# Later result functions, low parts on GpSimd and later mean matmuls in a hybrid encoder layer

## The chip, the cores and the metric

The kernel runs on one core of one Trainium2 chip. The metric is the device time of one execution in microseconds (us). A core has five engines with a queue of instructions each: TensorE (PE in the profile; its weight loads are PEld), VectorE (DVE), ScalarE (ACT), GpSimd (POOL) and SyncE (SP). Each engine works through its own queue in order. Where an instruction needs what another engine or a transfer makes, it waits on a semaphore, and all that stands behind it in the same queue waits too. DMA transfers are issued from queues of SP and GpSimd and run beside the engines.

## What is computed

One encoder layer is applied to two groups of tokens with shared weights: a prompt of 512 tokens and a sample of 1024, both 1024 channels wide, all in float32. Cut to its core:

```python
mod = jax.nn.silu(c) @ w_ada + b_ada
shift, scale, gate = jnp.split(mod[:, None, :], 3, axis=-1)
h = rms_norm(x, g_pre) * (1 + scale) + shift
a_val, a_glu, a_z, u, v, b_z, g_a, g_b = jnp.split(h @ w_in, IN_SPLITS, axis=-1)
# conv branch: GLU, depthwise conv of 31 taps, LayerNorm, gates, projection
y_a = (silu(layer_norm(conv(a_val * sigmoid(a_glu)) + conv_b)) * silu(a_z)) @ conv_proj
# spatial gating branch: per chunk of 128 tokens and channel group
v = layer_norm(gelu(v)); mixed = einsum("gpq,bnqgc->bnpgc", w_s, v) + b_s
y_b = (gelu(u) * mixed * silu(b_z)) @ sgu_proj
m = sigmoid(g_a) * y_a + sigmoid(g_b) * y_b
return x + gate * rms_norm(m @ w_out, g_post)
```

## The kernel before

**Matrix products in three passes.** Every operand of a large product is split into a high part (a rounded copy, `hi`) and a low part (what is left, `lo`), and each product is three matmuls: hi by hi, hi by lo, lo by hi. A weight unit is a tile of 128 x 1024. It is loaded by SP into one of four `raw` buffers; ScalarE copies it into `hi` (line 247). The low part is made in one of two ways. With `by_dma` set, ScalarE writes the negated weight into `lo` (line 250), GpSimd issues a DMA that adds the raw weight to it (line 240), and the `raw` buffer is free when that DMA has landed. Without it, VectorE subtracts (line 259, `unit_dve`). For `hi`, and for `lo` too, there is a ring of four buffers.

**Steps.** The work of TensorE is a list of steps, `steps`, run in the order of the list. A plain step is 24 matmuls of 512 columns. Steps 0 to 87 are the prompt (`CONV_END = 88`): input columns, v (steps 16 to 23), u, the gates, the projections and, as the last eight, the output product with w_out (`steps_o`). Steps 88 to 103 are v of the two sample halves `sa` and `sb` (`steps_v`). Then come 28 pairs of column blocks of the sample, seven steps of 12 matmuls each (`pair`). From step 300 on follow the projections of the sample halves with sproj (`post_B`, two times eight steps), then cproj (`post_A`) and the output (`steps_o`) of each half. The unit's way of making its low part is chosen where the step is made: in `col_step` (line 495), `steps_v` (line 529) and `steps_o` (line 589).

**A pair.** For two column blocks of both halves, seven products of half depth replace eight, in the Winograd form of Strassen's scheme. They go into three banks of PSUM: X (products 0, 2, 4 and 6), Y (product 1) and Z (products 3 and 5). Banks X and Z are added to without being cleared, so what they hold in between is copied out: ScalarE copies X after products 0, 2 and 4 and Z after product 3 (`snap`, line 1014). A product that adds to a bank must wait until the copy of it is done. VectorE adds the copies into three of the four results: C11 after product 1 (line 1018), C22 after product 4 (line 1022), C12 after product 5 (line 1026); the fourth, C21, stays in X. The caller's `finish` applies a sigmoid, GELU or SiLU to a result on ScalarE (lines 1126, 1131, 1148, 1153) and stores it to HBM (`spill`), or, for "um" and "hB", multiplies it on VectorE with an operand that has been stored before (`mul`, line 1158) and is requested some products ahead (`ask`, line 1142). The first eight pairs make the input of the sample's conv (`pair_glu`), whose end is handed over in `finish("end")`.

**The order on the engines.** The order is written out by a planner in the kernel. For each step `s` it emits what follows the step before it, `p`, in this order: `p.a1` (ScalarE: copies or functions), ScalarE's splits of later weights, some background work of VectorE, `p.d1` (VectorE), `p.a2` (ScalarE, after `d1`), background work, `p.d2`, VectorE's splits, then the matmuls of the step, loads of raw weights, `st.extra` (requests), and background work up to the step's end. Before the change a function of C11, C22 or C12 is in `a2` of the product that completes the result, so it stands on ScalarE ahead of the copy in `a1` of the next product. Background work (`bg`, `fill`) is the conv's taps (line 403, 31 for each of eight blocks of the sample, 128 x 1024 each), the normalisations and the splits of their results. The planner keeps a clock for TensorE, VectorE and ScalarE with a cost for each instruction.

**Means.** A normalisation needs the mean over channels, which lie on partitions. `bcast_mean` splits a sum into hi and lo (lines 320 and 321) and multiplies both with a matrix of 1/1024 on TensorE (lines 331 and 332). These two matmuls are not steps; they are put between the matmuls of the steps by `pe_later` at the first place whose planned time is at least `LAG` (1.0 us) after the planned end of the operand. The places are the start of a step and the middle of a plain one (`poll`). After the conv, `late_ln` loads its result again, normalises each sample half and makes hA, the operand of `post_A`: ScalarE's line 1241 makes its high parts, VectorE's line 1232 its low parts. hB, the operand of `post_B`, is made by `hB_gen` (lines 1269 and 1274).

Of the kernel before, what the change touches and what calls it, by code (L numbers as in the profile page):

```python
# [17 lines left out]
F32 = mybir.dt.float32  # L18
# [3 lines left out]
ALU = mybir.AluOpType  # L22
# [18 lines left out]
LAG = 1.0  # L41
PLAIN = 5.25
PROD = PLAIN / 2
CONV_END = 88
# [36 lines left out]
def layer_kernel(ctx: ExitStack, tc, x_p, x_s, xt_p, xt_a, xt_b, par, w_blk, w_v, cproj, sproj, w_out, w_ada, w_gate, wsT, bs,  # L81
# [121 lines left out]
    steps = []  # L203
# [38 lines left out]
    def unit_act(u):  # L242
        if u.hi is None:
            have(u)
            u.hi = part_tile("hi")
            u.lo = part_tile("lo")
            S.copy(u.hi, u.raw)  # L247
            clk["act"] += 0.96
            if u.by_dma:
                S.activation(u.lo, u.raw, AF.Copy, scale=-1.0)  # L250
                clk["act"] += 0.96
                lo_by_dma(u.lo, u.raw)
                u.raw = True
                live["raw"] -= 1
# [50 lines left out]
    def pe_later(lag, cost, fn):  # L305
        box = {}

        def go(now):
            box["b"] = fn()
            box["t"] = now  # L310
        pe_items.append((clk["dve"] + lag, cost, go))
        return box
# [12 lines left out]
    def bcast_mean(src):  # L325

        hi, lo = yield from parts(src)

        def go():
            b = bank()  # L330
            PE.matmul(b, lhsT=onemr, rhs=hi, start=True, stop=False)
            PE.matmul(b, lhsT=onemr, rhs=lo, start=False, stop=True)
            return b
        box = pe_later(LAG, 0.43, go)
        yield from ready(box)
        return box["b"]

# [154 lines left out]
        return st  # L492

    def col_step(t, src, act, a1=None, d1=None, d2=None, a2=None, pre=None, box=None, need=None, by_dma=True):
        u = Unit(src, len(steps), by_dma and (len(steps) < CONV_END or len(steps) % 2 == 0))

        def mm():
            b = bank()
            mm_cols(b, u, act())
            box[0] = b  # L500

        st = add_step(Step(mm, a1, d1, a2, d2, pre, need=need), u)

        def quarter(b, wh, wl, q):
            box[0] = b
            mm_quarter(b, wh, wl, act(), q)
        st.quarter = quarter
        return st
# [15 lines left out]
    def steps_v(t, need=None):  # L524

        for h in range(2):
            banks = []
            for kc in range(4):
                u = Unit(w_v[h, kc], len(steps), len(steps) % 2 == 0)

                def mm(u=u, kc=kc, banks=banks):
                    if kc == 0:
                        banks[:] = [bank() for _ in range(4)]
                    mm_rows(banks, u, t.operand(), kc)

                def a1(h=h, banks=banks):
                    if h == 0:
                        t.v = t.v_home()
                        t.bn = smp.tile([P, 4, 12], F32, tag="bn", name="bn", bufs=1)
                    for i in range(4):  # L540
                        S.activation(t.v[:, i, h * T:(h + 1) * T], banks[i], AF.Gelu_apprx_tanh)

                def d1(h=h):
                    for i in range(4):
                        dv(0.65, lambda: V.bn_stats(out=t.bn[:, i, h * 6:h * 6 + 6], in_=t.v[:, i, h * T:(h + 1) * T]))

                def d2(h=h):
                    if h == 0:
                        return
                    mv = smp.tile([P, 4, 2], F32, tag="mv", name="mv")  # L550
                    for i in range(4):
                        dv(0.15, lambda: V.bn_aggr(out=mv[:, i, :], in_=t.bn[:, i, :].rearrange("p (c s) -> p c s", s=6)))
                    var = smp.tile([P, 4], F32, tag="ss", name="var")
                    dv(0.1, lambda: V.tensor_copy(var, mv[:, :, 1]))
                    r = rstd_small(var, 4, LN_EPS)
                    for i in range(4):
                        dv(0.65, lambda: V.tensor_scalar(t.v[:, i, :], t.v[:, i, :], mv[:, i, 0:1], r[:, i:i + 1],
                                                         op0=ALU.subtract, op1=ALU.mult))
                    if t.after_v:
                        t.after_v()  # L560
                last = kc == 3
                add_step(Step(mm, a1 if last else None, d1 if last else None, None, d2 if last else None,
                              act=2.2 if last else 0.0, need=need if h == 0 and kc == 0 else None), u)
# [20 lines left out]
    def steps_o(t, final, on_end=None):  # L584

        for h in range(2):
            banks = []
            for kc in range(4):
                u = Unit(w_out[h, kc], len(steps), len(steps) < CONV_END or len(steps) % 2 == 0)

                def mm(u=u, h=h, kc=kc, banks=banks):
                    if kc == 0:
                        banks[:] = [bank() for _ in range(4)]
                    if final and h == 1 and kc >= 1:
                        t.wl.append(u)
                        if kc == 3:
                            for i in range(4):
                                for c in (1, 2, 3):
                                    mm_rows(banks, t.wl[c - 1], t.m, c, (i,))
                        return  # L600
                    mm_rows(banks, u, t.m, kc)

                def a1(h=h, kc=kc, banks=banks):
                    if kc == 3:
                        if h == 0:
                            t.o = tok(slot())
                            t.q = smp.tile([P, 2, 4], F32, tag="q", name="q")
                        junk = wk()
                        for i in range(4):
                            S.activation(junk, banks[i], AF.Square, scale=1.0 / 32, accum_out=t.q[:, h, i:i + 1])  # L610

                def d1(h=h, kc=kc, banks=banks):
                    if kc == 3:
                        if h == 1 and final:
                            out_last(t, banks)
                            return
                        c = slice(h * T, h * T + T)
                        for i in range(4):
                            dv(0.6, lambda: V.tensor_mul(t.o[:, i, c], banks[i], G[t.g][:, c]))
                        if h == 1:  # L620
                            bg.insert(0, out_gen(t))
                st = add_step(Step(mm, a1, d1, act=2.3 if kc == 3 else 0.0), u)
                if h == 0 and kc == 0:
                    def start():
                        out_load(t)
                        t.o_begun = True
                    st.extra = start
# [361 lines left out]


    pairs = []

    def pair(src1, src2, finish):

# [16 lines left out]
        def snap(name, of):  # L1011
            def a1():
                st[name] = wk()
                S.copy(st[name], st[of])  # L1014
            return a1
# [16 lines left out]
        mul = getattr(finish, "mul", None)  # L1032
        ask = getattr(finish, "ask", None)

        def times(*what):
            return (lambda: [mul(x) for x in what]) if mul else None

        prod("X", "a", 0, (0, 0), True, False, a1=snap("p1", "X"))
        prod("Y", "a", 1, (0, 1), True, True, d1=d_c11, a2=lambda: finish("C11", st), act=0.0)
        prod("X", "b", 0, "S2", False, False, a1=snap("u2", "X"), d1=times("C11"), need="S")  # L1040
        prod("Z", "b", 1, "S1", True, False, a1=snap("s5", "Z"))
        prod("X", "c", 0, "S3", False, False, a1=snap("u3", "X"), d1=d_c22, a2=lambda: finish("C22", st))
        prod("Z", "c", 1, "S4", False, True, d1=d_c12, a2=lambda: finish("C12", st), need="S4", act=0.0)
        steps[-1].d2 = times("C22")
        prod("X", "d", 0, (1, 1), False, True, a1=lambda: finish("C21", st),
             d1=times("C12", "C21") or (lambda: finish("end", st)))
        if ask:
            for i, what in ((1, ("C11",)), (3, ("C22",)), (4, ("C12", "C21"))):
                steps[i0 + i].extra = lambda what=what: [ask(x) for x in what]


# [658 lines left out]
    for s in range(NH, n + 1):  # L1710
# [7 lines left out]
            clk["pe"] += st.dur  # L1718
        pe1 = clk["pe"]
        clk["act"] = max(clk["act"], pe0)  # L1720
        if p.a1:
            p.a1()
            clk["act"] += p.act
        events(s, "act")
        fill(pe0 + 0.5)
        if p.d1:
# [2 lines left out]
        if p.a2:  # L1729
            p.a2()  # L1730
            clk["act"] = max(clk["act"], clk["dve"]) + 0.6
        fill(pe1 - 1.5, 2)
        if p.d2:
            p.d2()
        events(s, "dve")
# [80 lines left out]
```

## Time and profile before

| | us |
|---|---|
| median of 3 runs | 1467.63 |
| lowest and highest | 1466.49, 1473.89 |
| the profiled execution | 1466.83 |
| its span, first to last instruction | 1464.9 |
| TensorE busy | 1432.5 |
| VectorE busy | 1129.0 |
| ScalarE busy | 742.3 |
| GpSimd busy | 186.2 |

The span is that of the only core. Busy is the time in which an engine has at least one instruction under way; successive matmuls overlap, so TensorE counts as busy while its matmuls follow one another closely. In a row of a timeline the first number is the start in us from the span's start, the second the duration, then come engine, line, operation, what is written and read, the shape and the count; in brackets stands the idle time of the engine just before, and what ended it. In a row of groups the last numbers are the busy time in us, the mean of one instruction in ns, and the idle time before them. L1014 is line 1014 of the kernel. An instruction of a queue that issues a DMA is marked SPq or POOLq.

### The profile page before, as it was taken

What the parts mean: (1) busy time and instruction counts of PE and PEld (TensorE: products, weight loads), DVE (VectorE), ACT (ScalarE), POOL (GpSimd) and SP (SyncE); (2) the same over time, 40 slices, a digit from 0 to 9 for tenths busy, and PEclk for the clock granted to TensorE, in tenths of its full rate; (3) what the DMA queues carried; (4) which work ended last, traced back from release to release, by engine and by line L of the source; (5) the groups of instructions that cost most, each with busy time, mean ns of one, the idle gap of its engine ahead of it and who ended that gap; (6) DMA issues with size and microseconds to landing.
All of it is one profiled execution on the core that took longest, in us unless ns stands there. A gap on an engine that the chain in (4) does not pass through costs nothing.

```text
span 1464.9 us, 17769 instructions
## 1 busy us (share of the span) xinstructions
PE 1432.5 (98%) x6332; PEld 1169.3 (80%) x6332; DVE 1129.0 (77%) x1596; ACT 742.3 (51%) x1064; POOL 186.2 (13%) x220
## 2 busy tenths in 40 slices
PE   8999999999999989999999999999999989999997
PEld 4688888888888878888888888877888867888886
DVE  6769999976356455867999898898999939587645
ACT  3532544553486454454545565555556545554442
POOL 0000111111111110011111111111111100000000
PEclk9999999999999999999999999999999999999999
DMA  9266787897999998967666878877977799878782
GB/s 342 79 215 182 198 201 166 203 256 181 279 266 244 284 263 272 281 168 201 155 158 166 209 194 242 255 211 218 256 192 191 194 307 276 265 222 237 211 269 72
DMA packets 120040, 321.68 MB, mean 220 GB/s; under 512 B 13328, under 2 KB 17040, under 8 KB 119184
## 3 DMA queue, kind: packets, MB, share of 16 engines
q1 hardware_dynamic: 88992, 229.85, 45.2%
q0 software_dynamic: 30960, 90.72, 33.7%
q8 instruction: 49, 0.80, 0.2%
q14 instruction: 39, 0.32, 0.1%
HBM read 182.10 MB, written 47.71 MB: 157 GB/s over the span
## 4 chain that ended last, share of the span: by engine, by line
PE 80%; DMA 11%; DVE 4%; issue 2%; ACT 2%; SPq 1%; DVEq 0%; ACTq 0%; POOLq 0%
PE b L451 11%; PE b L449 11%; PE b L450 11%; PE b L483 10%; PE b L484 10%; PE b L485 10%; PE b L473 4%; PE b L474 4%; PE b L472 4%; DMA lo<-raw 2%; DMA wk<-d 2%; PE b L568 1%; DMA raw<-in_w_blk_dram 1%; DMA raw<-in_sproj_dram 1%; DVE c L403 1%
## 5 line engine op out<-in xcount | busy, mean ns | idle before, releaser
L483 PE MATMUL b<-A,hi 128*128 128x512 f32 x784 | 306.8, 391 | 6.9 <-ACT wk L1014 6.9
L484 PE MATMUL b<-A,hi 128*128 128x512 f32 x784 | 305.8, 390 | 0.0
L485 PE MATMUL b<-A,lo 128*128 128x512 f32 x784 | 305.7, 390 | 0.0
L449 PE MATMUL b<-A,hi 128*128 128x512 f32 x776 | 303.7, 391 | 0.0
L451 PE MATMUL b<-A,lo 128*128 128x512 f32 x776 | 302.8, 390 | 0.2 <-DMA lo<-raw 0.2
L450 PE MATMUL b<-A,hi 128*128 128x512 f32 x776 | 302.8, 390 | 0.0
L403 DVE SCALAR_TENSOR_TENSOR c<-c,prm 128x1024 f32<-128x1024 f32 x240 | 297.3, 1278 | 0.6
L247 ACT CAST hi<-raw 128x1024 fp32r<-128x1024 f32 x145 | 152.0, 1048 | 262.4 <-DMA raw<-in_w_v_dram 61.7
L240 POOL DMA_DIRECT2D lo<-raw x131 | 113.4, 865 | 788.8 <-ACT lo L250 690.8
L483 PEld LDWEIGHTS b<-A,hi 128*128 128x128 f32 x784 | 147.6, 188 | 40.1 <-ACT wk L1014 9.7
L485 PEld LDWEIGHTS b<-A,lo 128*128 128x128 f32 x784 | 147.6, 188 | 30.5
L484 PEld LDWEIGHTS b<-A,hi 128*128 128x128 f32 x784 | 147.5, 188 | 30.6 <-DVE A L967 0.2
L451 PEld LDWEIGHTS b<-A,lo 128*128 128x128 f32 x776 | 146.1, 188 | 31.3 <-DMA lo<-raw 0.7
L449 PEld LDWEIGHTS b<-A,hi 128*128 128x128 f32 x776 | 146.1, 188 | 30.4 <-issue 0.2
L450 PEld LDWEIGHTS b<-A,hi 128*128 128x128 f32 x776 | 146.0, 188 | 30.5 <-issue 0.2
L403 DVE SCALAR_TENSOR_TENSOR S<-c,prm,S 128x512 f32<-128x512 f32 x240 | 162.6, 745 | 0.2
L473 PE MATMUL b<-lo,A 128*128 128x512 f32 x384 | 150.6, 392 | 5.0 <-DMA lo<-raw 5.0
L472 PE MATMUL b<-hi,A 128*128 128x512 f32 x384 | 150.8, 393 | 0.0
L474 PE MATMUL b<-hi,A 128*128 128x512 f32 x384 | 150.0, 391 | 0.0
L240 POOL DMA_DIRECT2D lo<-T x84 | 72.4, 862 | 456.7 <-ACT lo L1068 374.0
L1014 ACT COPY wk<-b 128x512 f32<-128x512 f32 x112 | 65.0, 585 | 121.2 <-PE b L485 117.5
L250 ACT ACTIVATE lo<-raw 128x1024 fp32r<-128x1024 f32 x103 | 108.7, 1055 | 0.0
(206 smaller groups left out, 1630.7 us busy)
## 6 DMA issues: line engine op xcount, KB each, us to landing
raw<-in_w_blk_dram SPq DMA_DIRECT2D x105, 512.0 KB, 5.6
lo<-raw POOLq DMA_DIRECT2D x103, 512.0 KB, 6.6
d<-wk SPq DMA_DIRECT2D x142, 256.0 KB, 3.7
wk<-d SPq DMA_DIRECT2D x116, 256.0 KB, 5.9
lo<-T POOLq DMA_DIRECT2D x28, 512.0 KB, 5.7
lo<-T POOLq DMA_DIRECT2D x56, 256.0 KB, 4.4
raw<-in_w_v_dram SPq DMA_DIRECT2D x24, 512.0 KB, 5.6
raw<-in_sproj_dram SPq DMA_DIRECT2D x24, 512.0 KB, 6.1
```

What stands on the lines that cost most here:

```text
L240: GP.dma_start(lo.bitcast(F32), src, accum_op=ALU.add)
L247: S.copy(u.hi, u.raw)
L403: lambda: V.scalar_tensor_tensor(acc, in0=win, scalar=wt, in1=acc, op0=ALU.mult, op1=ALU.add))
L449: PE.matmul(dst, lhsT=wh3[:, k, :], rhs=hi, start=(k == 0), stop=False)
L450: PE.matmul(dst, lhsT=wh3[:, k, :], rhs=lo, start=False, stop=False)
L451: PE.matmul(dst, lhsT=wl3[:, k, :], rhs=hi, start=False, stop=(k == NK - 1))
L472: PE.matmul(banks[i], lhsT=hi, rhs=wh3[:, kk, :], start=(k == 0), stop=False)
L473: PE.matmul(banks[i], lhsT=hi, rhs=wl3[:, kk, :], start=False, stop=False)
L474: PE.matmul(banks[i], lhsT=lo, rhs=wh3[:, kk, :], start=False, stop=(k == NK - 1))
L483: PE.matmul(dst, lhsT=wh3[:, k, :], rhs=hi, start=st, stop=False, skip_group_check=True)
L484: PE.matmul(dst, lhsT=wh3[:, k, :], rhs=lo, start=False, stop=False, skip_group_check=True)
L485: PE.matmul(dst, lhsT=wl3[:, k, :], rhs=hi, start=False, stop=sp, skip_group_check=True)
```

## The change

The diff has four parts.

- In a pair, the function of C11, C22 or C12 is no longer emitted in `a2` of its product but put on a list (`late["act"]`) that is emitted one product later, right after that product's `a1`. The multiplications of "um" and "hB" and the end of a GLU pair are put on a second list (`late["dve"]`), which VectorE gets one product after the function, ahead of `d2`. The requests for the stored operands are made one product later.
- A unit's `by_dma` has a third value, "gp": GpSimd subtracts `hi` from `raw` into `lo`, without ScalarE's negation and without the DMA. From step 88 on, every second unit that was made by DMA is made in this way.
- Before step 88, all units of the prompt's v are made by DMA; before, every second one was made by VectorE.
- The matmuls of a mean are requested `2 * LAG`, 2.0 us, after their operand.

```diff
@@ unit_act
-            if u.by_dma:
+            if u.by_dma == "gp":
+                GP.tensor_tensor(out=u.lo, in0=u.raw, in1=u.hi.bitcast(F32), op=ALU.subtract)
+                u.raw = True
+                live["raw"] -= 1
+            elif u.by_dma:
                 S.activation(u.lo, u.raw, AF.Copy, scale=-1.0)
@@ bcast_mean
-        box = pe_later(LAG, 0.43, go)
+        box = pe_later(2 * LAG, 0.43, go)
@@ col_step
-        u = Unit(src, len(steps), by_dma and (len(steps) < CONV_END or len(steps) % 2 == 0))
+        u = Unit(src, len(steps), by_dma and (len(steps) < CONV_END or (len(steps) % 2 == 0 and "gp")))
@@ steps_v
-                u = Unit(w_v[h, kc], len(steps), len(steps) % 2 == 0)
+                u = Unit(w_v[h, kc], len(steps), True if len(steps) < CONV_END else len(steps) % 2 == 0 and "gp")
@@ steps_o
-                u = Unit(w_out[h, kc], len(steps), len(steps) < CONV_END or len(steps) % 2 == 0)
+                u = Unit(w_out[h, kc], len(steps), True if len(steps) < CONV_END else len(steps) % 2 == 0 and "gp")
@@ pair
+    late = {"act": [], "dve": []}
+
+    def turn(kind):
+        fns, late[kind] = late[kind], []
+        for f in fns:
+            f()
...
-        def times(*what):
-            return (lambda: [mul(x) for x in what]) if mul else None
+        def after_next(what):
+
+            def act():
+                finish(what, st)
+                if mul:
+                    late["dve"].append(lambda: mul(what))
+            late["act"].append(act)
+
+        def c21():
+            finish("C21", st)
+            if mul:
+                late["dve"].append(lambda: mul("C21"))
+
+        def end():
+            late["dve"].append(lambda: finish("end", st))
...
-        prod("Y", "a", 1, (0, 1), True, True, d1=d_c11, a2=lambda: finish("C11", st), act=0.0)
-        prod("X", "b", 0, "S2", False, False, a1=snap("u2", "X"), d1=times("C11"), need="S")
+        prod("Y", "a", 1, (0, 1), True, True, d1=d_c11, a2=lambda: after_next("C11"), act=0.0)
+        prod("X", "b", 0, "S2", False, False, a1=snap("u2", "X"), need="S")
...
-        prod("X", "c", 0, "S3", False, False, a1=snap("u3", "X"), d1=d_c22, a2=lambda: finish("C22", st))
-        prod("Z", "c", 1, "S4", False, True, d1=d_c12, a2=lambda: finish("C12", st), need="S4", act=0.0)
-        steps[-1].d2 = times("C22")
-        prod("X", "d", 0, (1, 1), False, True, a1=lambda: finish("C21", st),
-             d1=times("C12", "C21") or (lambda: finish("end", st)))
+        prod("X", "c", 0, "S3", False, False, a1=snap("u3", "X"), d1=d_c22, a2=lambda: after_next("C22"))
+        prod("Z", "c", 1, "S4", False, True, d1=d_c12, a2=lambda: after_next("C12"), need="S4", act=0.0)
+        prod("X", "d", 0, (1, 1), False, True, a1=c21, d1=end)
         if ask:
-            for i, what in ((1, ("C11",)), (3, ("C22",)), (4, ("C12", "C21"))):
+            for i, what in ((2, ("C11",)), (4, ("C22",)), (5, ("C12", "C21"))):
@@ the loop over steps
+        muls, late["dve"] = late["dve"], []
         if p.a1:
             p.a1()
             clk["act"] += p.act
+        turn("act")
         events(s, "act")
...
         fill(pe1 - 1.5, 2)
+        for f in muls:
+            f()
         if p.d2:
             p.d2()
```

## The prediction

> **What bounds the kernel now.** I read the totals first, then who TensorE waits for, then the engines' busy time per 20 us, and last the timelines around the largest gaps. Totals and waits:
>
> ```profile
> span 1464.9 us, 17769 instructions
> PE 1432.5 (98%) x6332; PEld 1169.3 (80%) x6332; DVE 1129.0 (77%) x1596; ACT 742.3 (51%) x1064; POOL 186.2 (13%) x220
> PE b L483 <- ACT wk L1014: 6.9, 6, 2.1
> PE b L473 <- DMA lo<-raw: 5.0, 4, 2.6
> PE b L331 <- ACT wk L320: 4.1, 2, 2.6
> ```
>
> TensorE is the bound: busy 98%, idle 1464.9 - 1432.5 = 32.4 us. No matmul is removed, so the change can only win idle time and what follows it. The three wait rows (us in total, times, longest) hold 16.0 us of that, and each answers to one part of the diff. Three windows of 20 us (TensorE, weight loads, VectorE, ScalarE, GpSimd, then granted clock, DMA share, GB/s):
>
> ```profile
> 900.00:920.00 20.00, 20.00 (x90) 16.57 (x89) 17.18 (x21) 10.80 (x17) 3.46 (x4) 1.00 0.94 275
> 1160.00:1180.00 20.00, 17.87 (x72) 14.30 (x72) 15.90 (x17) 12.48 (x21) 3.44 (x4) 0.91 1.04 293
> 1220.00:1240.00 20.00, 18.26 (x72) 14.38 (x72) 18.51 (x30) 9.43 (x13) 1.86 (x2) 0.91 0.79 203
> ```
>
> A full stretch holds 90 matmuls, 0.22 us each. Two stretches with a stall hold 72 at clock 0.91, so each lost 18 x 0.22 = 4.0 us, more than the idle time in it: matmuls just after a stall ran at half pace. Every stall also costs about 0.16 us beyond its row, since a matmul lasts 0.39 us but the next one normally starts after 0.22.
>
> **Part 1: the functions.** The worst of five like stalls of the products, on VectorE, ScalarE and TensorE:
>
> ```profile
> 1013.27 0.69 DVE L1158 TENSOR_TENSOR wk<-wk 128x512 f32<-128x512 f32 x1 [1.33 <-DMA wk<-d]
> 1013.88 4.87 DVE L403 SCALAR_TENSOR_TENSOR c<-c,prm 128x1024 f32<-128x1024 f32 x4
> 1018.66 0.68 DVE L1018 TENSOR_TENSOR wk<-b,wk 128x512 f32<-128x512 f32 x1
> ```
>
> ```profile
> 1019.38 0.63 ACT L1148 ACTIVATE wk<-wk 128x512 f32<-128x512 f32 x1 [5.18 <-DVE wk L1018]
> 1019.92 1.06 ACT L1014 COPY wk<-b 128x512 f32<-128x512 f32 x2
> ```
>
> ```profile
> 1020.53 0.50 PE L483 MATMUL b<-A,hi 128*128 128x512 f32 x1 [1.80 <-ACT wk L1014]
> ```
>
> VectorE is held by a multiplication that waits for its spilled operand (L1158), then has four conv taps in its queue, and makes C11 late (L1018). C11's function (L1148) stands in ScalarE's queue ahead of the copy of the X bank (L1014), idles ScalarE 5.18 us, and the fifth product can't write X until that copy is done. The change puts the function behind this copy. The copy needs only product three, long done, so TensorE starts at about 1020.53 - 1.80 = 1018.7. What is late next: the function still runs at 1019.4 and the copy of Z behind it ends at 1020.5; Z is written again one product later, at 1018.7 + 12 x 0.22 = 1021.3. So 0.8 us are left in the worst pair.
>
> Five of the six stalls are of this kind: 6.9 - 2.13 (the sixth, below) = 4.8 us idle, plus 5 x 0.16, is 5.6 us. I take 5.0, because a stall that goes no longer lets VectorE catch up, and 0.8 us isn't much. The bounds are 0 and 5.6.
>
> The sixth is another kind:
>
> ```profile
> 1172.09 1.05 ACT L247 CAST hi<-raw 128x1024 fp32r<-128x1024 f32 x1 [3.45 <-DMA raw<-in_sproj_dram]
> 1173.05 1.05 ACT L250 ACTIVATE lo<-raw 128x1024 fp32r<-128x1024 f32 x1
> 1174.01 0.61 ACT L1126 ACTIVATE wk<-wk 128x512 f32<-128x512 f32 x1
> 1174.53 1.12 ACT L1269 CAST A<-wk 128x512 fp32r<-128x512 f32 x2
> 1175.55 1.06 ACT L1014 COPY wk<-b 128x512 f32<-128x512 f32 x2
> ```
>
> ```profile
> 1176.18 0.61 PE L483 MATMUL b<-A,hi 128*128 128x512 f32 x1 [2.13 <-ACT wk L1014]
> ```
>
> ScalarE waits for a weight load and the X copy stands behind it. The late weight stays, but the negation L250 (0.96 from start to start) goes to GpSimd and the function L1126 (0.52) moves behind: about 1.5 us of the 2.13. This window lost 4.0 us in all, 1.7 of it matmuls at half pace after the stall. I take 3.0 back; the bounds are 0 and 4.0.
>
> The gate multiplications also move one product later, and so do the requests for their operands (same count on SP), so the lead of the loads stays or grows; the stores of the functions' results keep their count and their place behind the function. The buffers are held one product, 2.6 us, longer, and the end of each GLU pair hands its conv input over as much later. I cost these at nothing: VectorE has room between the first conv and the last (461.26 busy of 496.00 us, below). Without that cover the cost would be 2.6 us, once.
>
> ```profile
> 680.00:1176.00 496.00, 489.27 (x2152) 403.03 (x2150) 461.26 (x497) 272.67 (x429) 88.82 (x103) 1.00 0.77 204
> 1185.00:1272.00 87.00, 82.48 (x353) 66.96 (x352) 58.88 (x91) 45.89 (x61) 7.02 (x8) 0.98 0.89 272
> 1272.00:1368.00 96.00, 96.00 (x424) 79.43 (x424) 67.23 (x99) 50.53 (x72) 7.79 (x9) 1.00 0.81 244
> ```
>
> **Part 2: low parts by GpSimd.** From step 88 on every second weight unit, 32 in all (8 of v, 24 after the products), loses ScalarE's negation and the accumulating DMA and gets one subtraction on GpSimd. The 4 odd v units of the prompt go the other way, from VectorE to negation and DMA.
>
> ```profile
> L250 ACT ACTIVATE lo<-raw 128x1024 fp32r<-128x1024 f32 x103 | 108.7, 1055 | 0.0
> L240 POOL DMA_DIRECT2D lo<-raw x131 | 113.4, 865 | 788.8 <-ACT lo L250 690.8 <-DVE S L403 18.3 <-DMA raw<-in_cproj_dram 14.5
> lo<-raw POOLq DMA_DIRECT2D x103, 512.0 KB, 6.6
> L259 DVE TENSOR_TENSOR lo<-raw,hi 128x1024 fp32r<-128x1024 f32 x42 | 51.3, 1221 | 41.8 <-ACT hi L247 41.3
> L192 POOL TENSOR_SCALAR_AFFINE_SELECT ident<-ones 128x128 f32<-128x128 f32 x1 | 0.3, 287 | 0.6 <-DVE ones L188 0.6
> ```
>
> And the two places where a sample v unit's low part is waited for:
>
> ```profile
> 527.99 1.05 ACT L247 CAST hi<-raw 128x1024 fp32r<-128x1024 f32 x1 [2.37 <-DMA raw<-in_w_v_dram]
> 540.33 0.50 PE L473 MATMUL b<-lo,A 128*128 128x512 f32 x1 [1.67 <-DMA lo<-raw]
> 584.61 0.50 PE L473 MATMUL b<-lo,A 128*128 128x512 f32 x1 [0.44 <-DMA lo<-raw]
> ```
>
> The trace has no such subtraction on GpSimd. From below it costs VectorE's 1.22 us; from above, eight times the one 128x128 operation that GpSimd does, 8 x 0.287 = 2.3 us, or more, since that one has a single input. I take 2.3. The old way costs 1.06 + 0.87 + 6.6 = 8.5 us from hi to lo, so up to there a slower GpSimd is no loss. The first sample v unit has hi at 529.0, so lo would be there at 531.3 against a need at 540.33 - 1.67 = 538.7. Both stalls go: 1.67 + 0.44 + 2 x 0.16 = 2.4 us. The rest of the 5.0 in the wait row is in the prompt's output steps, before step 88, and stays. On GpSimd's queue the subtraction waits for hi where the DMA issue waited for the negation; behind it stand the next units' low parts, and GpSimd is 13% busy. The raw buffer is freed some 6 us earlier, and weight loads that wait for it start earlier; I count nothing for that. The 4 prompt units cost ScalarE 1.06 and GpSimd 0.87 each beside full TensorE windows: nothing, with a lead like that of their even neighbours.
>
> **Part 3: the means.** Two of twelve means stall TensorE:
>
> ```profile
> 1207.82 0.50 PE L331 MATMUL b<-wk,onemr 128*128 128x512 f32 x1 [2.55 <-ACT wk L320]
> 1208.55 0.50 PE L332 MATMUL b<-wk,onemr 128*128 128x512 f32 x1 [0.22 <-DVE wk L321]
> 1229.70 0.50 PE L331 MATMUL b<-wk,onemr 128*128 128x512 f32 x1 [1.52 <-ACT wk L320]
> ```
>
> The first costs 2.55 + 0.16 + 0.5 around its second matmul = 3.2 us, the second the 4.0 us of its window. Asked for 2 us ahead instead of 1, they move on TensorE only if the planner's next place for them, the start or the middle of a step, 12 matmuls or 2.6 us apart, changes: 1.0 / 2.6, some 4 times in 10. A mean that moves hides 2.6 us, all of its wait. The second's chances are better, since its request follows the first's result; but without the first stall TensorE also comes there 3 us sooner. Between 0 and 7.2 I take half, 3.6: the waits are as long as a half step, and neither end is nearer. The other ten means hold TensorE up nowhere; their chains get at most 2.6 us longer each, and what they feed is not waited for by any row of TensorE's waits.
>
> The slow stretches go with their stalls in this sum: 4.0 - 2.13 - 0.16 = 1.7 us at the sixth copy, and 4.0 - 1.52 - 0.16 - 0.5 = 1.8 at the second mean, half of it counted. In the rows, both windows with these stalls have the clock 0.91 and the full one 1.00. By the Trainium skill, "TensorE: Matmul & The Clock Gate", Part 1, it takes an idle window of about 3.4 us to lower the clock. By that rule stalls of 1.52 and 2.13 us would be too short, and the slow stretches might stay without them, which is a rival below.
>
> **Sum.** 5.0 + 3.0 + 2.4 + 3.6 = 14.0 us off the profiled execution. That one took 1466.83 us (span 1464.9 and 1.9 around it), 0.8 below the median 1467.63: 1466.8 - 14.0 = **1452.8 us**.
>
> **Rivals.**
>
> *GpSimd holds VectorE up.* Nearly all of VectorE's work between 1200 and 1232 has two inputs from SBUF. If GpSimd's subtraction keeps such an instruction waiting, the three units of those 32 us (one per two steps of 24 x 0.22 us) hold the chain of the second mean by up to 3 x 2.3 us, and the means' 3.6 us are not won. Then 1466.8 - 10.4 = 1456.4, and up to 1459.9 with half of these delays as stalls. This is the Trainium skill's rule in "SBUF — State Buffer", section "SBUF: two separate sides": an exclusive lock for a whole instruction; no run here shows it yet. For it: 18.51 busy of 20 on VectorE there. Against it: 87.00 - 58.88 = 28 us of the window to 1272 are idle.
>
> *The slow stretches stay.* If the half pace comes without the stalls, 1.7 + 0.9 = 2.6 us are not won: 1455.4. For it: 1.52 us of idle time is a short cause. Against it: the full window shows none.
>
> *The gain comes back at the means.* If the end of the conv does not come earlier with TensorE, TensorE arrives at the first mean 8 us sooner and waits there. For it: VectorE is 93% busy from 680 to 1176. Against it: the 35 us idle there. Won are the 2.4 of part 2: 1464.4.
>
> *The change does not do what it says*: VectorE falls back by more than the extra product, and the Z copy is late where the X copy was. Then parts 2 and 3 remain: 1466.8 - 6.0 = 1460.8.
>
> *Slower.* The same lock, and every one of the 8 to 9 subtractions per normalisation chain delays VectorE by its whole length. The last low parts of the two hA, and the first matmuls that read an hA:
>
> ```profile
> 1271.27 0.68 DVE L1232 TENSOR_TENSOR A<-wk,A 128x512 fp32r<-128x512 f32 x1
> 1281.34 0.39 PE L449 MATMUL b<-A,hi 128*128 128x512 f32 x1
> 1366.71 0.69 DVE L1232 TENSOR_TENSOR A<-wk,A 128x512 fp32r<-128x512 f32 x1 [2.07 <-ACT A L1241]
> 1369.40 0.39 PE L449 MATMUL b<-A,hi 128*128 128x512 f32 x1
> ```
>
> Each last block is read seven eighths into a step of 24 x 0.22 = 5.3 us. The second chain ends at 1367.4 and is read at 1374.0, 6.6 us to spare; the first at 1272.0 and 1286.0, 14.0, of which part 3 takes 3.6. Delays of 8 x 2.3 = 18.4 and 9 x 2.3 = 20.7 us (the windows above show 8 and 9 GpSimd instructions) would stall 8.0 and 14.1 us: 1452.8 + 22.1 = 1474.9. With d per subtraction the stalls are 8d - 10.4 and 9d - 6.6, so they begin at d = 0.7 and pass the 14.0 gained at d = 1.8. VectorE's idle 28 and 29 us in these windows speak against.
>
> **Chances.** Forecast 0.52, GpSimd holding VectorE 0.19, slow stretches staying 0.05, gain returned 0.12, not as said 0.05, slower 0.07. The range goes from all rows won, 5.6 + 4.0 + 2.4 + 7.2 = 19.2, 1447.6, opened to 1447.0, to the returned gain, 1464.4, and leaves out the slower case and errors at both ends. A measurement tells 0.5%, 7.3 us, from no change: below 1460.3 lie the forecast and the first two rivals, 0.76; within lie 0.17; slower 0.07.
>
> **What would show it.** In the changed profile, TensorE's waits for L1014's copy should be gone or under 2 us in sum, and C11's function should stand behind the X copy though L1018 is still up to 5 us late. The two waits for v's lo should go, while the prompt's (2.6 us at most) stays. GpSimd should show 32 subtractions of 1.2 to 2.5 us. If VectorE's mean for L1274 or L416 to L437 grows, the lock is real. Waits at L331 that are as long as before mean that the means did not move; a wait at L449 for hA would prove the slower case. I am wrong if the subtraction takes over 8 us, or if TensorE stops for something that has no row now.

## The result and the profile after

The changed kernel took 1461.2 us (median of six runs, 1459.88 to 1464.49) beside 1472.77 of the kernel before (six runs, 1466.49 to 1476.63): ratio 0.9932, interval 0.9913 to 0.9951. On a second chip the same comparison gave 0.9917 (0.9900 to 0.9934), 1458.92 against 1471.07. So the change wins some 10 to 12 us where 14.0 were forecast. The absolute 1452.8 is 8.4 us off, 5.9 of them because the forecast counted down from an execution of 1466.83 us, which turned out one of the fastest of the kernel before. As an absolute time 1461.2 lies nearer to 1460.8, which the prediction gave for a change that does not do what it says; the ratio to runs on the same chip and the traces tell the two apart.

Totals and TensorE's waits in the profile after. This execution, 1464.49 us, is the slowest of its six:

```profile
span 1462.7 us, 17703 instructions
PE 1433.6 (98%) x6332; PEld 1171.4 (80%) x6332; DVE 1170.1 (80%) x1592; ACT 715.9 (49%) x1036; POOL 245.4 (17%) x224
PE b L477 <- DMA lo<-raw: 4.6, 1, 4.6
PE b L487 <- ACT wk L1024: 3.8, 3, 2.9
PE b L336 <- DVE wk L325: 2.2, 2, 1.9
PE b L572 <- DVE c L561: 1.7, 4, 1.0
PE b L335 <- ACT wk L324: 0.8, 1, 0.8
```

Lines have moved: L1024 is the copy of a bank (was L1014), L335 and L336 are the two matmuls of a mean, L477 reads a low part of v or of the output weights, L572 is the mixing product after v. The three waits that held 16.0 us now hold 4.6, 3.8 and, for the means, 0.8 + 2.2 = 3.0. The wait at L572 is new: the sign that the prediction named for being wrong, at 1.7 us a small one. VectorE is busy 41 us longer with four instructions fewer. Two windows of the kernel before that the prediction does not show:

```profile
520.00:540.00 20.00, 18.21 (x72) 14.58 (x72) 6.57 (x10) 10.39 (x14) 2.32 (x3) 0.91 1.01 286
920.00:940.00 20.00, 19.80 (x88) 16.07 (x86) 17.01 (x20) 10.33 (x17) 3.44 (x4) 1.00 0.92 251
```

The same two in the changed kernel, and four of the windows of the prediction:

```profile
520.00:540.00 20.00, 17.44 (x70) 14.29 (x71) 10.18 (x13) 9.20 (x16) 4.19 (x3) 0.91 0.98 298
920.00:940.00 20.00, 17.11 (x63) 13.54 (x62) 17.72 (x21) 7.98 (x14) 2.61 (x3) 0.83 0.79 219
1160.00:1180.00 20.00, 20.00 (x90) 16.57 (x89) 18.92 (x19) 13.42 (x22) 6.02 (x5) 1.00 1.00 276
1220.00:1240.00 20.00, 20.00 (x89) 16.52 (x88) 19.19 (x28) 7.67 (x10) 5.32 (x2) 1.00 0.67 229
1185.00:1272.00 87.00, 85.12 (x369) 69.92 (x368) 72.04 (x92) 39.58 (x53) 20.70 (x8) 0.98 0.67 231
1272.00:1368.00 96.00, 96.00 (x425) 79.40 (x424) 83.49 (x103) 43.79 (x67) 22.39 (x9) 1.00 0.55 192
```

The stretches of the sixth copy and of the second mean (1160 and 1220) are full, at clock 1.00. New is 920 to 940, with 63 matmuls instead of 88, and 520 to 540 is no better (70, where it was 72). The place that lost 920 to 940, on VectorE, ScalarE and TensorE:

```profile
922.25 0.69 DVE L1179 TENSOR_TENSOR wk<-wk 128x512 f32<-128x512 f32 x1 [2.89 <-DMA wk<-d]
927.65 0.68 DVE L1028 TENSOR_TENSOR wk<-b,wk 128x512 f32<-128x512 f32 x1
```

```profile
921.23 0.59 ACT L1024 COPY wk<-b 128x512 f32<-128x512 f32 x1 [1.14 <-PE b L489]
928.36 0.63 ACT L1169 ACTIVATE wk<-wk 128x512 f32<-128x512 f32 x1 [6.55 <-DVE wk L1028]
928.90 0.57 ACT L1024 COPY wk<-b 128x512 f32<-128x512 f32 x1
```

```profile
929.52 0.79 PE L487 MATMUL b<-A,hi 128*128 128x512 f32 x1 [2.89 <-ACT wk L1024]
```

The first copy (of X, 921.23) runs as soon as its product ends, as the change wants it. Then the function of C11 (L1169) holds ScalarE 6.55 us, because the sum (L1028) is late behind a multiplication that waits for its load (L1179), and now the copy of Z (928.90) is what TensorE waits for. It is the 15th pair: C11 starts 9.3 us after the end of its product there, where it was 2.5.

### The profile page after: what moved, and what is told of

Same layout as the page of the kernel before. It is cut to its first block, busy times and chain, and to the rows that moved or that the text cites. A ratio compares the mean times of both kernels' runs of the same rounds, so it can differ in the third digit from the quotient of the medians.

```text
span 1462.7 us, 17703 instructions
## 1 busy us (share of the span) xinstructions
PE 1433.6 (98%) x6332; PEld 1171.4 (80%) x6332; DVE 1170.1 (80%) x1592; ACT 715.9 (49%) x1036; POOL 245.4 (17%) x224
## 4 chain that ended last, share of the span: by engine, by line
PE 70%; DMA 12%; DVE 10%; issue 3%; ACT 2%; SPq 2%; DVEq 0%; ACTq 0%
PE b L453 11%; PE b L454 11%; PE b L455 11%; PE b L489 8%; PE b L487 8%; PE b L488 8%; DMA wk<-d 5%; PE b L476 3%; PE b L477 3%; PE b L478 3%; DVE c L407 3%; DMA raw<-in_w_blk_dram 3%; DMA raw<-in_w_v_dram 2%; PE b L572 1%; DMA wk<-in_xt_a_dram 1%
## 5 line engine op out<-in xcount | busy, mean ns | idle before, releaser
L240 POOL DMA_DIRECT2D lo<-raw x103 | 89.0, 864 | 467.5 <-ACT lo L254 398.6
L477 PE MATMUL b<-lo,A 128*128 128x512 f32 x384 | 150.7, 392 | 4.6 <-DMA lo<-raw 4.6
L250 POOL TENSOR_TENSOR lo<-raw,hi 128x1024 fp32r<-128x1024 f32 x32 | 83.5, 2610 | 259.5 <-ACT hi L247 259.5
L1024 ACT COPY wk<-b 128x512 f32<-128x512 f32 x112 | 65.5, 585 | 124.6 <-PE b L489 116.9
```

The costliest lines, as they stand in the source:

```text
L240: GP.dma_start(lo.bitcast(F32), src, accum_op=ALU.add)
L477: PE.matmul(banks[i], lhsT=hi, rhs=wl3[:, kk, :], start=False, stop=False)
```

## The experiments

Each ratio is to the kernel before, on the same chip. The last column is (ratio - 1) times 1470 us. The rows come in three groups of four; those of a group share a chip, between groups the chips differ. Part 1 is the pairs, part 2 the low parts (with the prompt's v), part 3 the means.

| kernel | median us | ratio (interval) | us |
|---|---|---|---|
| all_again: the change | 1458.92 | 0.9917 (0.9900 to 0.9934) | -12.2 |
| p1_functions: part 1 alone | 1462.09 | 0.9939 (0.9921 to 0.9957) | -9.0 |
| p2_gpsimd: part 2 alone | 1466.06 | 0.9970 (0.9956 to 0.9983) | -4.4 |
| p3_means: part 3 alone | 1477.26 | 1.0037 (1.0020 to 1.0054) | +5.4 |
| no_means: parts 1 and 2 | 1460.10 | 0.9928 (0.9907 to 0.9948) | -10.6 |
| lo_memset | 1456.26 | 0.9905 (0.9884 to 0.9925) | -14.0 |
| prompt_out_gp | 1454.10 | 0.9887 (0.9867 to 0.9908) | -16.6 |
| early_ask | 1455.91 | 0.9900 (0.9880 to 0.9920) | -14.7 |
| p3_late | 1470.57 | 1.0010 (0.9992 to 1.0028) | +1.5 |
| no_gpsimd: parts 1 and 3 | 1473.01 | 1.0022 (1.0004 to 1.0040) | +3.2 |
| ask_out | 1448.67 | 0.9854 (0.9828 to 0.9880) | -21.5 |
| ask_out_late | 1443.89 | 0.9833 (0.9806 to 0.9860) | -24.5 |

### The parts, each alone

**The whole again** (no edit).

> The whole change once more, to have a second trace of it beside kernels of its parts on one chip. Theory A (the three parts each win what their stalls cost, less what comes back): 9 to 13 us faster than the kernel before, and the copy of Z is the place where TensorE waits in the products, 2 to 4 us in sum. Theory B (the one trace of after, 2.2 us shorter than the one of before, is typical): 0 to 4 us faster.

Theory A held: 12.2 us, and the copies are waited for 2.3 us in sum at five places. The 1464.49 us of the trace of after are not typical. Its waits for a copy, 3.8 us, are: the seven traces with the change's pairs and requests show 1.5 to 5.0.

**Part 1 alone.** The whole diff of `pair` and of the loop over steps; `LAG` and the three `Unit(...)` lines as before.

> Only the later functions, multiplications and requests of the pairs; low parts and means as before. Theory A: most of the gain is here, 5 to 8 us faster; waits for the X copy go to nothing. Rival: the waits only move from the copy of X to the copy of Z, one product later, because VectorE's sum C11 gets as much later as the multiplications now stand right ahead of it; then 0 to 3 us faster and a sum of 4 us or more at the Z copy.

9.0 us, a little above theory A's range. The copies are waited for 1.5 us in sum, where it was 6.9. The 6.9 were few: in the three other traces with the old pairs (part 2 alone, part 3 alone, the late means alone) it is 9.4 to 10.5.

**Part 2 alone.**

```diff
+            if u.by_dma == "gp":
+                GP.tensor_tensor(out=u.lo, in0=u.raw, in1=u.hi.bitcast(F32), op=ALU.subtract)
...
-                u = Unit(w_v[h, kc], len(steps), len(steps) % 2 == 0)
+                u = Unit(w_v[h, kc], len(steps), True if len(steps) < CONV_END else len(steps) % 2 == 0 and "gp")
```

The other two `Unit(...)` lines are edited likewise.

> Only the low parts by GpSimd from step 88 on and the prompt's v by DMA; functions and means as before. Theory A: the two stalls at v's low parts go and weight loads start earlier, 2 to 5 us faster, although VectorE is busy 40 us longer under GpSimd's subtractions. Rival (the lock on VectorE costs as much as it wins): between 1 us faster and 5 us slower, with new TensorE waits for VectorE in v's normalisation and at the means.

4.4 us, theory A, but the rival's sign is there too: a mean waits 3.5 us for VectorE. At v's low parts nothing is waited for any more; the 2.4 us that are left are one unit of the prompt's output.

**Part 3 alone.**

```diff
-        box = pe_later(LAG, 0.43, go)
+        box = pe_later(2 * LAG, 0.43, go)
```

> Only the means asked for 2 us after their operand. Theory A: the two stalls at the means after the products lose 2.6 us each and their slow stretches, 3 to 7 us faster. Rival: one or both of them do not move, or TensorE gets there earlier and waits again, and a mean of the prompt waits anew: within 2 us of the kernel before.

Neither: 5.4 us slower. TensorE's waits in this kernel:

```profile
PE b L473 <- DMA lo<-raw: 11.4, 5, 5.7
PE b L483 <- ACT wk L1014: 10.1, 6, 3.8
PE b L331 <- ACT wk L320: 2.0, 2, 1.4
```

The means themselves wait 2.0 us instead of 4.1. But low parts are waited for 11.4 us instead of 5.0, all between 500 and 548 us, 660 us before the means that the edit is for. ScalarE splits the sample's first operand (L873) there, first in the kernel before and then in this one:

```profile
477.28 1.39 ACT L873 ACTIVATE A<-wk,s_t 128x512 fp32r<-128x512 f32 x2 [1.42 <-DVE wk L869]
```

```profile
487.50 1.34 ACT L873 ACTIVATE A<-wk,s_t 128x512 fp32r<-128x512 f32 x2
```

And who holds SP's queue between 480 and 548, before and then in this kernel:

```profile
SPq L522 <- DVE wk L869: 30.1, 9, 10.9
```

```profile
SPq L522 <- DVE wk L869: 42.7, 9, 15.5
```

The sample's first operand comes 10 us later. The traces show the way there. Four of the early means make the gate of the output (`gate_gen`), one after the other, and the sample's norms start only behind the fourth. VectorE reads that one, before and in this kernel:

```profile
390.88 0.69 DVE L1680 SCALAR_TENSOR_TENSOR wk<-b,bg 128x512 f32<-128x512 f32 x1 [2.69 <-PE b L332]
```

```profile
399.88 0.69 DVE L1680 SCALAR_TENSOR_TENSOR wk<-b,bg 128x512 f32<-128x512 f32 x1 [5.07 <-PE b L332]
```

The second mean of a pair is read 5.9 us after the first in the kernel before and 8.7 here, a half step (2.7 us) more, and along the four that adds up to 9.0 us. It is so in every trace. In the six kernels whose early means are asked for after 1 us, the fourth is read at 387.2 to 391.3, the split starts at 476.4 to 477.9, and SP waits 23.6 to 30.1 us for the stores' operands; in the eight with 2 us it is 394.9 to 402.4, 483.3 to 491.1 and 37.5 to 44.5. The stores (L522) stand in SP's queue with the weight loads of the prompt's output and of v behind them: the first load of a weight of the sample's v is issued at 526.64 instead of 520.52. A late weight has no time left for the 8.5 us of negation and accumulating DMA. That this queue is what makes the low parts late is read from the traces; no run moved the stores alone.

**The late means alone.**

```diff
+    mlag = [LAG]
...
-        box = pe_later(LAG, 0.43, go)
+        box = pe_later(mlag[0], 0.43, go)
...
     def late_ln(t):
+        mlag[0] = 2 * LAG
```

> The kernel before, with the later request for the four means after the conv alone; the ten before it stay. The later means alone were 5 us slower, and their largest waits were at the prompt's output and the first v units, 600 us before the two means they are meant for. Theory (the harm is from the early means, which put off the sample's first operands and so hold SP's queue and the weight loads in it; the late ones help): 2 to 5 us faster than the kernel before. Rival (the later request after the conv is harm or of no effect by itself): within 2 us or slower.

The theory's second half fell: 1.5 us slower, its interval takes in no change. The late means, for which the request is later, win nothing by themselves. The two waits are still there, 2.7 us in sum instead of 4.1, and that execution lost more elsewhere. 1.0037 with the early means and 1.0010 without them point to these as the harm, but the intervals overlap and the chips differ. Stronger is that the split starts at 477.7 here, as before, and the last run below.

### What the parts are worth within the whole

**Without part 3**, the whole with `pe_later(LAG, ...)`.

> The change without its third part: functions and GpSimd's low parts, means asked for 1 us after their operand. Alone, the later means were 5 us slower than the kernel before, by waits for accumulating DMAs at the prompt's output and the first v units. Theory A (GpSimd's low parts cover that harm, and the later means help after the products): 1 to 4 us slower than the whole change, that is 8 to 11 us faster than the kernel before. Rival (the later means are harm in the whole change too): 13 to 17 us faster than the kernel before, faster than the whole change.

10.6 us, within theory A's 8 to 11 and short of the rival's 13. But it is 0.9928 beside 0.9917 of the whole, on another chip, and the intervals overlap, so within the whole part 3 is not told from nothing. One thing is clear: the 5 us of harm that it does alone isn't there.

**Without part 2**, the whole with the three `Unit(...)` lines as before.

> The change without its second part: functions and means later, low parts as before. Functions alone were 9.0 us faster, means alone 5.5 us slower, GpSimd's low parts alone 4.4 us faster, the whole 12.2 us faster. Theory (GpSimd's low parts take away the harm of the early means, so the parts do not add): 2 to 5 us faster than the kernel before, that is GpSimd's part is worth 7 to 10 us within the whole. Rival (the parts add, and the means' harm alone was chance): 8 to 10 us faster.

3.2 us slower than the kernel before, where even the theory had 2 to 5 us faster. Functions alone win 9.0 us; with the later means added and the low parts by DMA nothing is left of that. The window from 500 to 560, in the kernel before, without part 2, in the whole, and in ask_out_late below:

```profile
500.00:560.00 60.00, 55.42 (x236) 44.71 (x235) 30.33 (x47) 27.45 (x42) 5.16 (x6) 0.97 0.96 277
```

```profile
500.00:560.00 60.00, 51.64 (x210) 41.19 (x209) 28.31 (x45) 29.47 (x44) 6.88 (x8) 0.94 0.96 279
```

```profile
500.00:560.00 60.00, 55.42 (x237) 45.22 (x236) 30.85 (x43) 21.94 (x37) 11.58 (x7) 0.97 0.82 246
```

```profile
500.00:560.00 60.00, 60.00 (x266) 49.68 (x265) 42.13 (x54) 27.31 (x43) 18.03 (x7) 1.00 0.68 232
```

Full speed is 266 matmuls in 60 us. Without GpSimd's low parts, and with the early means later, 56 are missing; in the whole, 29, and in the kernel before, 30. The DMA share is 0.96, 0.82 in the whole, and 0.68 where the prompt's output units are GpSimd's too. So part 2 is worth 4.4 us alone and about 15 (1.0022 against 0.9917, on two chips) beside parts 1 and 3. Some 5 to 6 us of that are in this window, where it covers harm of part 3 (27 matmuls against this trace of the whole, 21 against the second one); the rest was not followed.

### What GpSimd's subtraction costs

**The same without reading SBUF.** GpSimd writes zeros, so the low parts of these 32 units are left out.

```diff
-                GP.tensor_tensor(out=u.lo, in0=u.raw, in1=u.hi.bitcast(F32), op=ALU.subtract)
+                GP.memset(u.lo.bitcast(F32), 0.0)
```

> The whole change, with GpSimd's subtraction replaced by a memset of the low part: the low parts of 32 weight units are left out (zero), the same instruction count, no read of SBUF by GpSimd. Theory lock (GpSimd's reading holds VectorE's two-input instructions): VectorE's busy time falls from 1170 us to about 1125, TensorE's waits for VectorE at the means (L336) and in v (L572) fall to under 0.5 us in sum, and the kernel is 2 to 5 us faster than the whole change. Rival (VectorE is slower for another reason, or its delay is hidden): VectorE stays above 1150 us, or the time stays within 1 us of the whole change.

Rows of the subtraction in the profile after, and of its memset here; then VectorE's totals here:

```profile
L250 POOL TENSOR_TENSOR lo<-raw,hi 128x1024 fp32r<-128x1024 f32 x32 | 83.5, 2610 | 259.5 <-ACT hi L247 259.5
```

```profile
L250 POOL MEMSET lo<- 128x1024 f32 x32 | 31.1, 971 | 296.4 <-PE b L455 158.2 <-PE b L477 127.9 <-PE b L489 10.3
PE 1432.0 (98%) x6332; PEld 1170.0 (80%) x6332; DVE 1124.9 (77%) x1592; ACT 716.2 (49%) x1036; POOL 192.5 (13%) x224
```

The lock is real: VectorE's busy time falls from 1170 to 1124.9 us with the same 1592 instructions, 45 us by 32 subtractions, 1.4 each. In the profile after it can be seen directly, on GpSimd and VectorE:

```profile
1242.28 2.59 POOL L250 TENSOR_TENSOR lo<-raw,hi 128x1024 fp32r<-128x1024 f32 x1 [7.94 <-ACT hi L247]
```

```profile
1242.66 2.77 DVE L165 SCALAR_TENSOR_TENSOR wk<-wk 128x512 f32<-128x512 f32 x1
```

VectorE's instruction, 0.69 us in the kernel before, starts 0.4 us after GpSimd's and ends 0.6 us after it. This agrees with the Trainium skill, "SBUF — State Buffer", section "SBUF: two separate sides", in both halves: an instruction with two SBUF inputs waits for the whole of a GpSimd instruction that reads SBUF, and not for one that only writes. The time says less: 0.9905 against the whole's 0.9917 on another chip, 2 us, with intervals that overlap, so that theory and rival are not told apart by it. The memset does not wait for `hi` either, so the lock's own price can be smaller still. TensorE's waits at the means' second matmul go from 2.2 to 0.3 us, and those after v (L572), 1.7 us, are gone. So VectorE loses 45 us and the kernel a few at most, since VectorE has room where these units are.

### The stalls that were left

**The prompt's output units by GpSimd too.**

```diff
-                u = Unit(w_out[h, kc], len(steps), True if len(steps) < CONV_END else len(steps) % 2 == 0 and "gp")
+                u = Unit(w_out[h, kc], len(steps), "gp" if len(steps) < CONV_END else len(steps) % 2 == 0 and "gp")
```

> The whole change, and the eight weight units of the prompt's output (steps 80 to 87) get their low parts from GpSimd too. Theory (the largest stall that is left, 4.6 us and the slow stretch behind it, is the accumulating DMA of those units): this wait goes and the kernel is 4 to 7 us faster than the whole change, 16 to 19 us faster than the kernel before. Rival (the late weight load is behind it, and TensorE waits for hi, or for VectorE, instead): within 2 us of the whole change.

The wait is gone, and the kernel is 1454.1 us, ratio 0.9887 against the whole's 0.9917 on another chip, 4.4 us: the theory, at its lower end, though the intervals still overlap by 0.0008.

**Requests at the old places.**

```diff
-            for i, what in ((2, ("C11",)), (4, ("C22",)), (5, ("C12", "C21"))):
+            for i, what in ((1, ("C11",)), (3, ("C22",)), (4, ("C12", "C21"))):
```

> The whole change, with the stored operands of the multiplications requested at the old places, one product earlier than the change has them. Theory (VectorE's lag of 5 to 9 us behind TensorE comes from multiplications that wait for these loads): its waits for wk<-d go down from about 7 us in sum to under 3, the lag stays under 5 us, no wait at the copy of Z, 1 to 3 us faster than the whole change. Rival (the loads are late since the stores ahead of them on SP wait for VectorE, or buffers run short): same waits, within 1 us.

VectorE's waits of the multiplications between 800 and 1176 us, in the kernel before, in the change and here:

```profile
DVE wk L1158 <- DMA wk<-d: 7.0, 7, 1.9
```

```profile
DVE wk L1179 <- DMA wk<-d: 16.6, 11, 3.6
```

```profile
DVE wk L1179 <- DMA wk<-d: 7.8, 5, 3.5
```

The old places halve these waits, though not to the 3 us that the theory had. The 7.0 of the trace before are again few: the other three traces with the old pairs show 9.4 to 12.1. All seven with the new pairs and the later requests show 12.0 to 16.8, the three with the old places 3.4 to 7.8, and the waits for a copy go with them: 1.5 to 5.0 us in the seven, 0 to 1.1 in the three. From the 17th pair on the sum C11 starts 0.1 to 4.3 us after its product here, up to 7.1 in the whole; in the 15th pair it is 7.3 here and 6.6 to 11.0 in the seven. The kernel is 0.9900, 2.5 us ahead of the whole, though the intervals overlap.

**Both**, and **both with the late means alone**: the two edits above, the second with that of p3_late.

> The whole change, with the stored operands requested one product earlier and the prompt's output low parts by GpSimd. Alone, on top of the change, these gave some 1.6 and 3.4 us. If they are separate causes: 16 to 19 us faster than the kernel before, no wait over 1 us at lo or at the copy of Z. If they share a cause: 14 to 16.

> As ask_out, with the later request only for the four means after the conv. If the early means are harm even where GpSimd makes the low parts: 1 to 3 us faster than ask_out, and no wait at the prompt's mean (1 to 2 us at L335 and L336 in the traces of the change). If that harm was covered: within 1 us of ask_out.

The two edits are separate causes: 21.5 us together, more than the theory's range, with a wait of 1.4 us at lo that the theory did not allow. Keeping the early means where they were gives 1443.89 us (1443.39 to 1447.42) beside 1448.67 (1446.33 to 1450.04) on the same chip, 4.8 us by the medians and 3.3 by the means, where 1 to 3 were expected: the early means asked for later are harm even where GpSimd makes the low parts. TensorE's waits in ask_out_late, without those of the kernel's start:

```profile
span 1441.9 us, 17691 instructions
PE b L338 <- DVE wk L325: 2.3, 2, 1.7
```

No wait for a bank's copy, for a low part or for a weight is left, and TensorE is busy 1424.0 of 1441.9 us. It was idle 32.4 us in the kernel before and is 17.9 here; the other 8.5 us of the span are busy time that went with the stalls, though no matmul did.

## Why the prediction came out as it did, step by step

**The bound** was right: TensorE, and only what follows its waits can be won. The last kernel above wins 24.5 us, more than the 19.2 that the prediction named as all its rows. Part of the difference is the prompt's output stall, which lay outside the diff; part is that 24.5 counts from the median of the kernel before and 19.2 from a fast execution (from span to span it is 23.0).

**Part 1 (8.0 forecast, 9.0 measured alone, 6.3 to 11.6 by the interval).** The mechanism was right, with the X copy running at once. "What is late next" was right too, the copy of Z, and so was its size: in the prediction's worst pair C11 starts 5.4 us after its product and 0.8 us are left, 6.2 in all; in the 15th pair of the change it starts 9.3 us after and the wait is 2.89, so 6.4 were free. The step that failed is the cost of nothing for requests: "the lead of the loads stays or grows". The multiplications' waits for these loads went from 7.0 to 16.6 us, and C11 came some 2 us later on average from the 17th to the 26th pair (4.9 us after its product, where it was 3.1). That used up the 0.8 us: 3.8 us of waits in one trace, 2.3 in another, and 0.6 with the old requests. That 9.0 were won all the same is in part luck: the rows that the 8.0 were counted from hold less than other traces of the old pairs, 6.9 us of waits for a copy and not 9.4 to 10.5. (The 3.0 for the sixth copy also counted on part 2, which takes the negation away.)

**Part 2 (2.4 forecast, 4.4 measured alone).** The two v stalls went. The subtraction takes 2.61 us, where 2.3 was taken and 2.5 named as the most. The raw buffer that is free earlier, counted as nothing, and a DMA share of 0.84 instead of 0.96 from 500 to 560 us may explain the surplus; they were not tried apart, and neither were the prompt's v units that went to DMA.

**Part 3 (3.6 forecast, 5.4 slower measured alone).** This step failed. The working of the two late means was fair in the place it looked at: their waits fell from 4.1 us to 2.0 alone and 1.9 in the whole, whose other 1.1 us at means are at an early one. The sentence "The other ten means hold TensorE up nowhere; ... what they feed is not waited for by any row of TensorE's waits" is where it went wrong. The prediction gave every chain "at most 2.6 us longer", and that is what one mean costs, 2.7; but four of them stand one behind the other in the gate, and the fourth comes 9.0 us later, and with it the norms. The norms give the stores in SP's queue, with the weight loads behind them. TensorE's row for that says "DMA lo<-raw", 5.0 us, and it was in the prediction, read as a fixed stall of the prompt; with part 3 alone it is 11.4. Within the whole, GpSimd's low parts cover most of this harm.

**The sum** was 14.0; the measured 10 to 12 contain 9.0 and 4.4 of parts 1 and 2, and a part 3 that is about nothing instead of 3.6. That no term stands alone (part 3 is 5.4 us slower alone, part 2 is worth 4.4 or 15) was not in it. So the sum came out near by luck: part 3 was wrong in its sign, and part 2 happened to cover it.

**The rivals.** GpSimd does hold VectorE up, by the mechanism named, with 1.4 us per subtraction, and the mean of L1274 (now L1295) went from 685 to 920 ns, as the prediction said it would. Of the time, some 2 us come from it, not told from nothing. The slower case did not come, though by its own formula it should have: at 1.4 us per subtraction it gives 0.8 + 6.0 us of stalls, and TensorE waits for hA nowhere. The formula put the whole delay on hA. VectorE had idle time to take it up, busy 72.04 of 87 and 83.49 of 96 us in the windows of the chains, and the last low parts of the two hA end at 1273.5 and 1366.3, where they ended at 1272.0 and 1367.4. "The gain comes back at the means" is seen in parts 1 and 2 alone, where a mean waits 3.5 us in each (for ScalarE and for VectorE); in the whole it is out, with 3.0 us at the means. "Not as said" was right in its mechanism for a few pairs only. "The slow stretches stay" is out at 1160 and 1220, which are at clock 1.00 without their stalls; new ones came with new stalls, 0.83 from 920 to 940 with the 2.89 us before 929.52. By the Trainium skill, "TensorE: Matmul & The Clock Gate", Part 1, the clock falls after an idle window of about 3.4 us. The traces here show slow matmuls after shorter idle times: matmuls follow each other 0.43 us apart instead of 0.225 behind 2.89 us and, in the kernel before, 2.13 and 1.52 us of idle time.

## What to carry to other kernels

Ask of a delayed result not only whether an engine waits for it, but in which queue its store stands and which loads stand behind that store: this is how means asked for 1 us later came to cost up to 5.7 us at one low part. Ask, too, how many such delays stand one behind the other: four means, each up to 2.7 us later than the one ahead made it, came to 9.0. A low part, or any second product of a load, that costs 8.5 us of negation and DMA takes the slack from a late load; an engine that is 13% busy and makes it in 2.6 us gives that back, even if it slows a neighbour with room by 45 us. When a consumer is moved one product later, leave its request where it is.

## What was not expected of the hardware

- One GpSimd subtraction of 128x1024 lengthened VectorE's work by 1.4 us on average, and the wait shows as a longer instruction (0.69 to 2.77 us), not as idle time: busy time of VectorE went up by 41 us while its work went down.
- Matmuls after a stall of 2.89 us ran at half pace for some 6 us (63 of 90 in the window), and after one of 4.58 us for 3.5 us; a stall of this kind that is removed gives back more than its row.
- Executions of the same kernel differ by 10 us (1466.49 to 1476.63 in six), more than any one part of this change, and so do the waits in their traces. Only ratios of many runs on one chip, and what all the traces agreed on, told the parts apart.
